# Weight sums in DRAM handed out from the end of the first products, not in attention alone

## The chip, the cores and the metric

The kernel runs on one core of one Trainium2 chip. The metric is the device time in microseconds (us) of one execution. TensorE (PE, with its weight loads PEld) multiplies, VectorE (DVE), ScalarE (ACT) and GpSimd (POOL) work on tiles, and SyncE (SP) issues most of the transfers. POOL issues the others, all those that add to what lies at their destination. PE and SP follow the order in which the program is written, in all of the kernel. In the stretch that this change touches, DVE, ACT and POOL do so too. An instruction that waits holds up everything that stands behind it on its engine.

## The reference, cut to what matters

One layer with sliding-window attention, an output projection, and a gated embedding, for 512 tokens of width 2048:

```python
hn = rmsnorm(x, norm_g)
q, k, v, gate = split(hn @ w_in)         # 32 heads of 64, 4 key/value heads
s = q @ k.T * 64 ** -0.5 + bias          # window of 128 keys; bias by distance, 32 buckets, from rel_bias
m = max(s.max(-1), sink)                 # one more score per head, the "sink"
p = exp(s - m) / (exp(s - m).sum(-1) + exp(sink - m))
x = x + ((p @ v) * silu(gate)) @ w_out
emb = p_in @ ple_proj
x = x + emb * sigmoid(rmsnorm(x, ple_norm) @ ple_gate)
out = rmsnorm(x, final_g)
```

## The kernel before, in words

**Products.** Every large product is done as three matmuls on a high and a low part (`mm3`, lines 126 to 128). A piece of weights, 128 x 1024 numbers or 512 KB, is loaded by SP into a `wraw` tile (line 102), cast by ACT to its high part `whi` (line 109), and subtracted by DVE to its low part `wlo` (line 110). There are three buffers of each. The load of piece i+1 is issued when the split of piece i is handed out, and the load of piece 3 needs the buffer of piece 0, which is free when DVE has made `wlo` of piece 0.

**Stages.** First come the first products: 16 steps that make queries of the first two heads, all keys and values. `W.load(3)` and `W.get(0)` then load pieces 0 to 3 and split 0 to 2. `W.get(0)` ends with the load of piece 3 on SP. Behind it the program prepares keys and values, and POOL builds the table of biases: it loads `rel_bias` into `misc` (line 381), clears the table (382), fills it with 17 small copies (385, 390) and writes it to DRAM as `tdram` (392). SP reads the biases of the first heads back from `tdram` into a `bias` tile (`load_bias(0)`, line 444, four transfers). Then the projections run as a generator, one step of three matmuls (one of 16 parts of a product) at a time: 16 steps alone, and after that 64 blocks of attention between which the remaining steps are dealt out. A block is, in this order on the engines: two matmuls of scores (PE, line 462); on POOL, the sink into a column of the tile `t` (line 474) and a fill of masked places (477); on DVE, bias and scores added into `t` (482, 484 for the first two blocks) and the maximum taken (491); two exponentials on ACT (495); a reciprocal on DVE (497); a scaling on ACT into `pr` (506); one block later a transpose of `pr` on PE (515). The tile of scores has one buffer, so PE's scores of a block wait until DVE has read the scores of the block before. After attention come the output projection and the gated embedding (`ple_gate`).

**The sums.** Both late products use seven products in place of eight (sums of blocks of weights and of activations). The sums of weights are made in DRAM: a copy on SP (`copies`, line 662, DRAM to DRAM, 512 KB) and then an addition of another block into it on POOL (`adds`, line 664, 512 KB). There are 56 of each. `sum_weights(i)` does step i of 118: copy i/2 where i is even, and addition (i-1)/2 - 3 where i is odd, so an addition is handed out behind three copies later than its own. An addition waits on POOL for its copy to land. The first ten copies belong to `w_out` 7 (`small` twice, then eight pieces); their first use is in the output projection. Before the change each block of attention hands out its share of the 118 steps at the end of the block:

```python
for n in range(i * SUM_STEPS // blocks, (i + 1) * SUM_STEPS // blocks):
    sum_weights(n)
```

Of the kernel before, what the change touches and what calls it, by code (L numbers as in the profile page):

```python
# [11 lines left out]
F32 = mybir.dt.float32  # L12
F32R = mybir.dt.float32r
AF = mybir.ActivationFunctionType
ALU = mybir.AluOpType
# [5 lines left out]
P = 128  # L21
# [34 lines left out]
def trunk_kernel(ctx: ExitStack, tc: tile.TileContext, a: dict):  # L56
    nc = tc.nc
# [28 lines left out]
    WE = 1024  # L86
# [71 lines left out]
    def run(gen):  # L158
        for _ in gen:
            pass  # L160
# [34 lines left out]
    pre = ExitStack()  # L195
    start_pool = pre.enter_context(tc.tile_pool(name="start", bufs=3))

    front = ExitStack()
    for k in range(KC):
        if k == 0:  # L200
# [35 lines left out]
        if k == 0:  # L236
            first, second = slice(0, 1), slice(1, 2)
# [19 lines left out]
        f, e = k == 0, k == KC - 1  # L257
# [13 lines left out]
        for t in range(2):  # L271
            c = slice(t * P, (t + 1) * P)
            mm3(kt_ps[t], wh[:, c], wl[:, c], h, l, f, e)

        for part in "hl" if f else "lh":
            for t in range(NB):
                c = slice(t * P, (t + 1) * P)
# [6 lines left out]
        if 3 <= k < 3 + NB:  # L284
            t = k - 3
# [12 lines left out]
            nc.sync.dma_start(pn, a["ple_norm"])  # L298
    W.load(3)
    W.get(0)  # L300

    Q = {}

# [82 lines left out]
    for b in range(exact, BUCKETS):  # L386
        d = np.nonzero(bk == b)[0]
        if len(d):
            lo, n = P - 1 + int(d.min()), len(d)
# [37 lines left out]
    def first_chores(i, step):  # L427

        if step == 0 and i < NB - 1:
            make_diff(i + 1)  # L430
        if step and 1 <= i < NB:
            diffs[i][step - 1]()
        if step == 2 and 1 <= i - 1 < NB:
            spread_diff(i - 1)
        if step and 1 <= i - 2 < NB:
            split(V[i - 2], values[i - 2])[step - 1]()
# [71 lines left out]
    def turn(i):  # L508


        d, g = divmod(i, UNITS)
        pr = T.pop(i)
        pt = bank(f"pt{i}", "t")[:, :256]
        for u in range(2):
            nc.tensor.transpose(pt[:, u * P : (u + 1) * P], pr[:, u, :], ident)  # L515

        r = apool.tile([P, 2, 256], F32R, tag="r", name=f"r{i}", bufs=2)
        rh, rl = (r[:, l].rearrange("p (h u q) -> p u h q", h=4, u=2) for l in range(2))
        src = pt.rearrange("p (u h q) -> p u h q", u=2, h=4)
        nc.scalar.copy(rh, src)  # L520
        nc.vector.tensor_sub(rl, src, rh.bitcast(F32))  # L521
        yield
        own = None
        if g >= 2:
            own = apool.tile([P, 2, 256], F32R, tag="own", name=f"own{i}", bufs=2)
            rows = slice(0, P) if g % 2 else slice(0, HB)
            flat = lambda v: v[rows].rearrange("p l (u q) -> p (l u) q", q=HB)


            sign = -1 if g % 2 else 1  # L530
            nc.gpsimd.affine_select(  # L531
                out=flat(own), in_=flat(r).bitcast(F32), pattern=[[0, 8], [sign, HB]], compare_op=ALU.is_ge, fill=0.0,
                base=-HB - 1 if g % 2 else 0, channel_multiplier=-sign,
            )
        PT[i] = (r, own)
        yield
        if own is not None:
            here, there = slice(HB, P), slice(0, HB)
            if g % 2 == 0:
                here, there = there, here  # L540
            nc.scalar.copy(own[there, 0], own[here, 1].bitcast(F32))
# [85 lines left out]
        (4, 0): {0: 5, 1: 5, 2: 4, 3: 4}, (4, 1): {0: 3, 1: 3},  # L627
    }

    summed, copies, adds = {}, [], []

    def block(nm, r, c, jj, m):
        return a[nm][2 * (c - 1) + jj, 4 * (r - 1) + m]

    SUMS = [("w_out", 7), ("w_out", 5), ("w_out", 6), ("w_out", 4), ("ple_gate", 7), ("ple_gate", 5)]

    def small_block(r, c, m):

        return block("w_out", 2, 1, c - 1, 2 * (r - 1) + m)

    for (nm, p), small in zip(SUMS, (7, 5, 6, 4, None, None)):
        for m in range(2 if small else 0):
            t = summed["small", small, m] = tc.dram_tile([P, WE], F32, name=f"small_{small}_{m}")
            copies.append((t, {
                7: small_block(1, 2, m), 5: small_block(1, 1, m), 6: summed.get(("small", 7, m)),
                4: summed.get(("small", 6, m)),
            }[small]))
            adds.append((t, small_block(*{7: (2, 2), 5: (1, 2), 6: (1, 1), 4: (2, 1)}[small], m)))  # L650
        for jj in range(2):
            for m in range(4):
                t = summed[nm, p, jj, m] = tc.dram_tile([P, WE], F32, name=f"{nm}_{p}_{jj}_{m}")
                first = {7: (1, 2), 5: (1, 1)}.get(p)
                copies.append((t, block(nm, *first, jj, m) if first else summed[nm, {6: 7, 4: 6}[p], jj, m]))
                adds.append((t, block(nm, *{7: (2, 2), 5: (1, 2), 6: (1, 1), 4: (2, 1)}[p], jj, m)))
    SUM_STEPS = 2 * len(copies) + 6

    def sum_weights(i):

        if i % 2 == 0 and i // 2 < len(copies):
            nc.sync.dma_start(*copies[i // 2])
        elif i % 2 == 1 and 0 <= i // 2 - 3 < len(adds):
            nc.gpsimd.dma_start(*adds[i // 2 - 3], accum_op=ALU.add, max_dma_last_dim=8192)

    class Pieces:


# [70 lines left out]
    def add_stage(nm, order):  # L739
# [7 lines left out]
        for p in order:  # L747
            for jj in range(2):
# [5 lines left out]
                for m in range(4):  # L754
                    at[p, jj].append(len(B.specs))
                    if (nm, p) in SUMS:
                        src = summed[nm, p, jj, m]
# [90 lines left out]
    W.apart = True  # L848
    for n in range(KC):
        next(proj)  # L850
        if n % 4 == 3 and W.todo:
            W.todo.pop(0)()
    blocks = TWOS * UNITS
    left = KC * (len(kinds) - 1)

    def some(of, n=1):
        for _ in range(min(n, len(of))):
            of.pop(0)()

    softmax = iter(())  # L860
    for i in range(blocks + 3):

        before, softmax = softmax, scores(i) if i < blocks else iter(())
        turned = turn(i - 2) if 2 <= i < blocks + 2 else iter(())
        value = weigh(i - 3) if 3 <= i else iter(())
        next(turned, None)
        next(value, None)
        next(softmax, None)
        next(turned, None)
        next(before, None)  # L870
        next(softmax, None)
        first_chores(i, 0)
        if i in (6, 20, 36):
            idle.extend(make_key(1 + i // 16))
        todo = left // (blocks + 2 - i) if i < blocks + 2 else 0
        left -= todo
        for n in range(max(todo, 6)):
            if n < todo:
                next(proj)
            if n == 0:  # L880
                first_chores(i, 1)
                some(W.todo)
                some(chores or idle)
            elif n == 2:
                next(value, None)
                if len(chores) > 1:
                    some(chores)
            elif n == 3:
                next(turned, None)
                next(softmax, None)  # L890
            elif n == 4:
                first_chores(i, 2)
                some(chores or idle)
            elif n == 5:
                next(softmax, None)
        if i < blocks:
            for n in range(i * SUM_STEPS // blocks, (i + 1) * SUM_STEPS // blocks):
                sum_weights(n)
    for _ in proj:
        pass  # L900
    while chores or idle:
# [171 lines left out]
    for n, p in enumerate(ORDER_OUT):  # L1073
        nxt = out_forms.steps(ORDER_OUT[n + 1]) if n < 5 else iter(())
        for jj in range(2):
            later.extend(held.pop(waiting.get((p, jj)), ()))
            calls = iter(range(4))

            def between(m):
                q = small_steps.get((p, jj, m))  # L1080
                if q is not None:
                    next(small_made.setdefault(q, small_form(q)))
                q = SMALL.get((p, jj), {}).get(m)
                if q is not None:
                    small(q)

            def todo():
                step = next(calls)
                part = x_at.get((p, jj, step))
                if part is not None:  # L1090
                    load_x(part)
                next(nxt, None)
                if p == 4:

                    for _ in range({0: 2, 1: 2, 2: 2, 3: 2, 6: 2, 7: 2}.get(4 * jj + step, 0)):
                        turn(*turns.pop(0), "o")
                    if jj:
                        next(ple_first, None)

            ps = unit(p, jj, at_out, out_forms, todo, between)  # L1100
            posts = [partial_of(add_y, p, jj, tb, ps[tb]) for tb in range(2)]
            if p == 1:
                held[p, jj] = posts
            else:
                later.extend(posts)
        run(nxt)
        if p == 3:
            nc.sync.dma_start(fg, a["final_g"].partition_broadcast(P))
        if p == 3:
            turns = [(kp, th) for kp0, th in ((4, 1), (4, 0), (0, 0)) for kp in range(kp0, kp0 + 4)]  # L1110
# [144 lines left out]
    f = ple_forms.made[4]  # L1255
# [74 lines left out]
    n = done[3]  # L1330
# [87 lines left out]
```

## Time and profile before

| | us |
|---|---|
| median of 3 runs | 796.1 (795.71 to 797.07) |
| the profiled execution, its time | 794.62 |
| its span, first to last instruction | 792.9 |
| PE busy | 782.9 (99%) |
| DVE busy | 600.3 (76%) |
| ACT busy | 507.1 (64%) |
| POOL busy | 122.2 (15%) |

The granted TensorE clock of the profiled execution is 0.997. In the profile, SPq rows are transfers that SP issues, and "us to landing" of a transfer counts from its issue to the last of its 16 engines. The first products end near 71 us, the first block of attention starts near 82 us, and the output projection's first product starts near 440 us.

### The profile page before, as it was taken

The page shows a single profiled execution, that of the slowest core. Times are in us where ns is not written, and L with a number is a line of the kernel's source. Part 1 is how long each engine was busy: PE and PEld are TensorE (multiplying, and loading weights), DVE is VectorE, ACT ScalarE, POOL GpSimd, SP SyncE. Part 2 cuts the span into 40 slices and gives each one's busy share as a digit, 9 for nine tenths or more (in the row PEclk, how much of TensorE's full clock was granted, in tenths as well). Part 3 has the DMA queues.
Part 4 walks back from the last instruction along what each step waited for, and adds up shares of the span by engine and source line. Part 5 has one row for each costly group of instructions (what it writes and reads, how often), then busy time and mean ns, then how long its engine had stood idle before and what let it go on. Part 6 is the DMA issues. An engine that isn't in the chain of part 4 may idle for free.

```text
span 792.9 us, 11070 instructions
## 1 busy us (share of the span) xinstructions
PE 782.9 (99%) x3746; PEld 655.1 (83%) x3746; DVE 600.3 (76%) x1043; ACT 507.1 (64%) x1066; POOL 122.2 (15%) x246
## 2 busy tenths in 40 slices
PE   9999999999999999999999999999999999999995
PEld 8888888888888888888888888888888888888885
DVE  4546697877878687877777899778867757988896
ACT  6742576666767586666666654466698656656765
POOL 0020223131323213132222100000000120200000
PEclk9999999999999999999999999999999999999998
DMA  9883499899999989998997369767764995787633
GB/s 352 281 212 132 116 271 316 243 277 235 278 257 267 250 254 272 228 280 238 260 259 187 107 236 393 300 210 235 275 236 140 347 206 195 160 226 216 182 107 106
DMA packets 45577, 185.22 MB, mean 234 GB/s; under 512 B 6656, under 2 KB 7680, under 8 KB 40400
## 3 DMA queue, kind: packets, MB, share of 16 engines
q1 hardware_dynamic: 37984, 145.40, 52.2%
q0 software_dynamic: 7536, 39.12, 26.1%
q8 instruction: 29, 0.48, 0.3%
q14 instruction: 28, 0.23, 0.1%
HBM read 177.63 MB, written 62.97 MB: 303 GB/s over the span
## 4 chain that ended last, share of the span: by engine, by line
PE 91%; DVE 4%; DMA 2%; ACT 1%; issue 1%; ACTq 0%; SPq 0%; DVEq 0%
PE qps L126 7%; PE qps L128 7%; PE qps L127 7%; PE gps L126 7%; PE gps L128 7%; PE gps L127 7%; PE g L126 5%; PE g L127 5%; PE g L128 5%; PE o L127 4%; PE o L126 4%; PE o L128 4%; PE s L462 2%; PE vps L279 2%; DVE blo L701 2%; PE o L557 2%
## 5 line engine op out<-in xcount | busy, mean ns | idle before, releaser
L701 DVE TENSOR_TENSOR blo<-braw,bhi 128x1024 fp32r<-128x1024 f32 x102 | 124.3, 1221 | 40.9 <-ACT bhi L700 40.6
L700 ACT CAST bhi<-braw 128x1024 fp32r<-128x1024 f32 x102 | 107.1, 1051 | 70.0 <-PE o L128 23.6
L126 PE MATMUL gps<-xh,whi 128*128 128x512 f32 x256 | 99.8, 390 | 0.1
L128 PE MATMUL gps<-xh,wlo 128*128 128x512 f32 x256 | 99.9, 390 | 0.0
L127 PE MATMUL gps<-xl,whi 128*128 128x512 f32 x256 | 99.8, 390 | 0.0
L126 PE MATMUL qps<-xh,whi 128*128 128x512 f32 x224 | 87.7, 391 | 0.0
L128 PE MATMUL qps<-xh,wlo 128*128 128x512 f32 x224 | 87.5, 390 | 0.0
L127 PE MATMUL qps<-xl,whi 128*128 128x512 f32 x224 | 87.3, 390 | 0.0
L110 DVE TENSOR_TENSOR wlo<-wraw,whi 128x1024 fp32r<-128x1024 f32 x60 | 73.8, 1232 | 2.9 <-ACT whi L109 2.5
L126 PE MATMUL g<-bhi,fhg 128*128 128x512 f32 x192 | 75.1, 391 | 0.0
L127 PE MATMUL o<-blo,fho 128*128 128x512 f32 x192 | 74.8, 390 | 0.2 <-DVE blo L701 0.2
L126 PE MATMUL o<-bhi,fho 128*128 128x512 f32 x192 | 74.8, 390 | 0.0
L128 PE MATMUL g<-bhi,flg 128*128 128x512 f32 x192 | 74.8, 389 | 0.0
L128 PE MATMUL o<-bhi,flo 128*128 128x512 f32 x192 | 74.7, 389 | 0.0
L127 PE MATMUL g<-blo,fhg 128*128 128x512 f32 x192 | 74.7, 389 | 0.0
L531 POOL TENSOR_SCALAR_AFFINE_SELECT own<-r 64x512 fp32r<-64x512 f32 (+1 forms) x48 | 32.5, 677 | 245.6 <-DVE r L521 245.6
L520 ACT CAST r<-pt 128x256 fp32r<-128x256 f32 x64 | 23.8, 371 | 71.7 <-PE pt L515 71.3
L521 DVE TENSOR_TENSOR r<-pt,r 128x256 fp32r<-128x256 f32 x64 | 27.1, 424 | 55.8 <-ACT r L520 54.9
L109 ACT CAST whi<-wraw 128x1024 fp32r<-128x1024 f32 x60 | 62.3, 1040 | 5.4 <-issue 3.9
L128 PEld LDWEIGHTS gps<-xh,wlo 128*128 128x128 f32 x256 | 48.0, 188 | 10.1
L126 PEld LDWEIGHTS gps<-xh,whi 128*128 128x128 f32 x256 | 48.1, 188 | 9.4 <-PE vps L279 0.5
L495 ACT ACTIVATE t<-t,sm 128x129 f32<-128x129 f32 x128 | 50.6, 397 | 8.0 <-DVE sm L491 6.4
(224 smaller groups left out, 1740.8 us busy)
## 6 DMA issues: line engine op xcount, KB each, us to landing
wraw<-in_w_gate_in SPq DMA_DIRECT2D x32, 512.0 KB, 6.9
w_out<-in_w_out POOLq DMA_DIRECT2D x32, 512.0 KB, 8.6
braw<-w_out SPq DMA_DIRECT2D x32, 512.0 KB, 4.6
wraw<-in_w_q SPq DMA_DIRECT2D x28, 512.0 KB, 6.3
braw<-in_ple_gate SPq DMA_DIRECT2D x24, 512.0 KB, 3.4
braw<-in_w_out SPq DMA_DIRECT2D x22, 512.0 KB, 4.3
xw<-in_first SPq DMA_DIRECT2D x14, 640.5 KB, 6.3
w_out<-in_w_out SPq DMA_DIRECT2D x16, 512.0 KB, 8.5
```

The lines of the kernel that those rows point to most:

```text
L109: nc.scalar.copy(hi, raw)
L110: nc.vector.tensor_sub(lo, raw, hi.bitcast(F32))
L126: nc.tensor.matmul(ps, sh, mh, start=first, stop=False, skip_group_check=more)
L127: nc.tensor.matmul(ps, sh, ml, start=False, stop=False, skip_group_check=more)
L128: nc.tensor.matmul(ps, sl, mh, start=False, stop=last, skip_group_check=more)
L279: nc.tensor.matmul(v_ps[t], h[:, c], both[:, :, 256:512], start=f, stop=e, skip_group_check=True)
L495: nc.scalar.activation(su, su, AF.Exp, bias=sm[:, u : u + 1], accum_out=sm[:, 2 + u : 3 + u])
L520: nc.scalar.copy(rh, src)
L521: nc.vector.tensor_sub(rl, src, rh.bitcast(F32))
L531: nc.gpsimd.affine_select(out=flat(own), in_=flat(r).bitcast(F32), pattern=[[0, 8], [sign, HB]], compare_op=ALU.is_ge, fill=0.0, base=-HB ...
L700: nc.scalar.copy(hi, raw)
L701: nc.vector.tensor_sub(lo, raw, hi.bitcast(F32))
```

## The change

The functions and the lists move ahead of the first products, unchanged. The steps are then taken in order by `sum_some(n)` from one iterator: 8 steps behind `W.get(0)`, 8 steps during the 16 projection steps ahead of attention, 96 steps in attention's 64 blocks, and the last 6 one at a time in the output projection's first product.

```diff
+    sum_steps = iter(range(SUM_STEPS))
+
+    def sum_some(n):
+        for _, i in zip(range(n), sum_steps):
+            sum_weights(i)
 ...
     W.load(3)
     W.get(0)
+    sum_some(8)
 ...
     load_bias(0)
     W.apart = True
     for n in range(KC):
         next(proj)
+        if n % 2:
+            sum_some(1)
         if n % 4 == 3 and W.todo:
             W.todo.pop(0)()
 ...
         if i < blocks:
-            for n in range(i * SUM_STEPS // blocks, (i + 1) * SUM_STEPS // blocks):
-                sum_weights(n)
+            sum_some((i + 1) * (SUM_STEPS - 22) // blocks - i * (SUM_STEPS - 22) // blocks)
 ...
                 if part is not None:
                     load_x(part)
                 next(nxt, None)
+                sum_some(1)
                 if p == 4:
```

On the engines of the built kernel this gives the following. PE, DVE and ACT carry the same instructions in the same order as before. On SP, copies 0 to 3 stand between the load of piece 3 and the biases' four transfers. Copies 4 to 6 stand between those and the load of piece 4, copy 7 between the loads of pieces 4 and 5, and copies 8 and 9 ahead of that of piece 6. On POOL, addition 0 stands ahead of the load into `misc`, with which the table of biases begins. Additions 1 to 4 stand between the writing of `tdram` and the sink of the first block (line 474). The last three additions, 53 to 55, stand behind attention.

More of the change, by code (lines that the diff above doesn't have):

```diff
@@ L196, in trunk_kernel, with block, small_block, sum_weights @@
     start_pool = pre.enter_context(tc.tile_pool(name="start", bufs=3))
+    summed, copies, adds = {}, [], []
+    def block(nm, r, c, jj, m):
+        return a[nm][2 * (c - 1) + jj, 4 * (r - 1) + m]
+    SUMS = [("w_out", 7), ("w_out", 5), ("w_out", 6), ("w_out", 4), ("ple_gate", 7), ("ple_gate", 5)]
+    def small_block(r, c, m):
+        return block("w_out", 2, 1, c - 1, 2 * (r - 1) + m)
+    for (nm, p), small in zip(SUMS, (7, 5, 6, 4, None, None)):
+        for m in range(2 if small else 0):
+            t = summed["small", small, m] = tc.dram_tile([P, WE], F32, name=f"small_{small}_{m}")
+            copies.append((t, {
+                7: small_block(1, 2, m), 5: small_block(1, 1, m), 6: summed.get(("small", 7, m)),
+                4: summed.get(("small", 6, m)),
+            }[small]))
+            adds.append((t, small_block(*{7: (2, 2), 5: (1, 2), 6: (1, 1), 4: (2, 1)}[small], m)))
+        for jj in range(2):
+            for m in range(4):
+                t = summed[nm, p, jj, m] = tc.dram_tile([P, WE], F32, name=f"{nm}_{p}_{jj}_{m}")
+                first = {7: (1, 2), 5: (1, 1)}.get(p)
+                copies.append((t, block(nm, *first, jj, m) if first else summed[nm, {6: 7, 4: 6}[p], jj, m]))
+                adds.append((t, block(nm, *{7: (2, 2), 5: (1, 2), 6: (1, 1), 4: (2, 1)}[p], jj, m)))
+    SUM_STEPS = 2 * len(copies) + 6
+    def sum_weights(i):
+        if i % 2 == 0 and i // 2 < len(copies):
+            nc.sync.dma_start(*copies[i // 2])
+        elif i % 2 == 1 and 0 <= i // 2 - 3 < len(adds):
+            nc.gpsimd.dma_start(*adds[i // 2 - 3], accum_op=ALU.add, max_dma_last_dim=8192)
+    sum_steps = iter(range(SUM_STEPS))
+    def sum_some(n):
+        for _, i in zip(range(n), sum_steps):
+            sum_weights(i)
     front = ExitStack()
@@ L628, in trunk_kernel @@
     }
[L632 to L664, printed above, removed]
     class Pieces:
```

## The prediction

> **What bounds the kernel now.** I read the windows first, to see in which stage PE has time to give or none. The columns are each engine's busy us (and instructions), then the granted clock, the DMA share and GB/s.
>
> ```profile
> core 0: us, PE busy (x) PEld busy (x) DVE busy (x) ACT busy (x) POOL busy (x), PEclk, DMA share, GB/s
> 70.00:95.00 25.00, 24.93 (x114) 20.40 (x113) 18.19 (x39) 11.09 (x25) 6.12 (x11) 1.00 0.28 90
> 95.00:440.00 345.00, 345.00 (x1709) 290.43 (x1708) 266.62 (x589) 232.31 (x643) 89.97 (x182) 1.00 0.93 255
> 440.00:700.00 260.00, 259.72 (x1181) 215.08 (x1180) 205.16 (x236) 166.70 (x249) 15.93 (x18) 1.00 0.73 234
> 700.00:793.00 93.00, 84.13 (x400) 70.71 (x398) 76.00 (x115) 58.33 (x86) 3.44 (x4) 0.98 0.53 166
> ```
>
> PE is busy in every us of attention (95 to 440), although the DMA engines are at 0.93 there. From 70 to 700 it is idle for 0.07 + 0.00 + 0.28 = 0.35 us. The waits of PE, asked for next, say the same: after the start there is one.
>
> ```profile
> PE warm_ps L141 <- PEq L1408: 0.8, 1, 0.8
> PE o L127 <- DVE blo L701: 0.2, 1, 0.2
> ```
>
> So PE sets the time, at full clock, and nothing that lightens the transfers in attention can give back more than 0.35 us, unless it reaches the last stage with its 8.87 us of idle time, in which no sum of weights is made. Whatever delays PE anywhere is lost for good. The quiet stretch is 70 to 95: DMA share 0.28. The change moves work there. The question is whether something on which PE soon depends stands behind that work. I then followed SP and POOL instruction by instruction from 40 to 95 us, and from their landings to PE.
>
> **The change part by part.** *The fewer steps in attention* (96, not 118) and *the last three additions*, in the output projection on a POOL that is nearly idle (15.93 us busy in 260), remove nothing that PE waits for. I cost them at nothing: cover is PE's unbroken 345.00, and the last pieces, of `ple_gate`, are wanted only in the stage after.
>
> *The four copies behind the load of piece 3.* That load starts when DVE has finished the low part of piece 0:
>
> ```profile
> 56.68 1.23 DVE L110 TENSOR_TENSOR wlo<-wraw,whi 128x1024 fp32r<-128x1024 f32 x1 [1.79 <-ACT whi L109]
> 57.93 0.33 SPq L102 DMA_DIRECT2D wraw<-in_w_q  x1
> 62.55 1.72 SPq L444 DMA_DIRECT2D bias<-tdram  x4
> 64.37 0.84 SPq L102 DMA_DIRECT2D wraw<-in_w_q  x2
> 65.27 1.27 SPq L662 DMA_DIRECT2D small<-in_w_out  x2
> ```
>
> 57.93 + 0.33 gives 58.3 for copy 0, and at 1.27 / 2 = 0.63 each the four are issued by 60.8, before SP could start on the biases (62.55). On SP this costs nothing. What matters is when copy 0 lands, since POOL waits for it. Landings, in the order in which I use them (the last number is us from issue):
>
> ```profile
> w_out<-in_w_out SPq DMA_DIRECT2D x1, 512.0 KB, 4.0
> small<-in_w_out SPq DMA_DIRECT2D x2, 512.0 KB, 7.4
> small<-in_w_out POOLq DMA_DIRECT2D x1, 512.0 KB, 6.7
> ple_gate<-in_ple_gate POOLq DMA_DIRECT2D x1, 512.0 KB, 5.1
> w_out<-in_w_out POOLq DMA_DIRECT2D x32, 512.0 KB, 8.6
> misc<-in_rel POOLq DMA_DIRECT2D x1, 4.0 KB, 5.0
> tdram<-misc POOLq DMA_DIRECT2D x1, 48.0 KB, 5.3
> bias<-tdram SPq DMA_DIRECT2D x4, 20.0 KB, 1.8
> ```
>
> A copy alone took 4.0 (issued at 91.47), the two behind two loads 7.4. Copy 0 goes behind one load: I take the middle, 5.7, so it lands at 64.0 (62.3 to 65.7).
>
> *Addition 0 ahead of the table of biases.* Before, POOL did this:
>
> ```profile
> 44.20 0.53 POOL L381 DMA_DIRECT2D misc<-in_rel  x1
> 44.72 0.44 POOL L382 MEMSET misc<- 32x384 f32 x1
> 49.33 0.65 POOL L385 COPY misc<-misc 32x16 f32<-32x16 f32 x1 [4.17 <-DMA misc<-in_rel]
> 52.30 0.51 POOL L392 DMA_DIRECT2D tdram<-misc  x1 [0.29 <-DMA xw<-in_first]
> 62.60 0.18 POOL L474 COPY t<-sinkb 128x2 f32<-128x2 f32 x1 [9.78 <-PE vps L279]
> ```
>
> `tdram` was issued at 52.30 and landed at 57.6, five us before SP could use it. Now POOL waits at addition 0 until 64.0, and line 381, the memset, the 17 copies and line 392 all wait behind it. The load into `misc` moreover follows a 512 KB addition in POOL's one queue. That addition lands after 6.7 us (as the first one of attention, beside other traffic), at 70.7; between a lone one's 5.1 and the 8.6 median of attention it is 68.2 (there the 5.0 of `misc` itself ends last) to 74.3. `misc` lands just behind, at 70.9. From the landing of `misc` (44.20 + 5.0 = 49.2) to the issue of `tdram` (52.30) it took 3.1: 74.0. With its own 5.3, `tdram` lands at **79.3**. The ends: with 1.8, what a small transfer took in quiet, 68.2 + 3.1 + 1.8 = 73.1, and 74.3 + 0.2 + 3.1 + 5.3 = 82.9.
>
> *The load of piece 4.* SP waits for `tdram` at the biases, and behind them stand copies 4 to 6 and this load: 79.3 + 1.72 + 3 x 0.63 = 82.9 (76.7 to 86.5), where it was 64.4 before. How long it takes to land depends on what is in flight: three copies just ahead of it, and additions 1 to 3, which POOL issues right behind `tdram` as their copies have long landed. Its price:
>
> ```profile
> wraw<-in_w_q SPq DMA_DIRECT2D x2, 512.0 KB, 4.5
> wraw<-in_w_q SPq DMA_DIRECT2D x1, 512.0 KB, 8.2
> wraw<-in_w_q SPq DMA_DIRECT2D x1, 512.0 KB, 11.8
> q1 hardware_dynamic: 37984, 145.40, 52.2%
> q0 software_dynamic: 7536, 39.12, 26.1%
> ```
>
> 4.5 with nothing ahead (64.37), 8.2 behind a copy and small transfers beside an addition (106.55), 11.8 when the queues were full (108.02). I take 8.2: landing at **91.1**. The queues' totals agree: 145.40 MB in 52.2% of 792.9 us is 1.49 us per 512 KB on all engines, and 39.12 MB in 26.1% is 2.77 per addition. Three additions and four SP transfers are 8.3 + 6.0 = 14.3 us of work; begun at about 76 they end at 90. The ends are 76.7 + 4.5 = 81.2 and 86.5 + 11.8 = 98.3.
>
> *Who waits for piece 4.* ACT's cast of it stands ahead of the first exponentials, so everything of blocks 0 and 1 follows it:
>
> ```profile
> 81.85 1.05 ACT L109 CAST whi<-wraw 128x1024 fp32r<-128x1024 f32 x1 [3.89 <-issue]
> 83.23 1.50 DVE L110 TENSOR_TENSOR wlo<-wraw,whi 128x1024 fp32r<-128x1024 f32 x1
> 87.00 0.70 ACT L506 ACTIVATE pr<-t,sm 128x128 f32<-128x128 f32 x2 [0.23 <-DVE sm L497]
> 87.26 0.46 DVE L482 TENSOR_TENSOR t<-s,bias 128x96 f32<-128x96 f32 x2 [0.29 <-PE s L462]
> 87.63 0.45 DVE L484 TENSOR_TENSOR t<-s,t 128x96 f32<-128x96 f32 x2
> 91.84 0.38 PE L515 MATMUL pt<-ident,pr 128*128 128x128 f32 x2
> 91.97 0.39 PE L462 MATMUL s<-k,q 128*128 128x320 f32 x1
> ```
>
> From the cast's start, `pr` of block 0 is there 87.70 - 81.85 = 5.85 later, and the scores of block 1 are read 88.08 - 0.29 - 81.85 = 5.94 later (without the 0.29 spent waiting for PE). PE wants them at 91.84 and 91.97. So piece 4 may land as late as **86.0** for nothing, and each us beyond it stops PE for one. Piece 4 itself is multiplied later still.
>
> Sum: 91.1 - 86.0 = **5.1 us** at the transposes and scores near 92 us, then nothing more: DVE, with 18.19 us busy of 25, needs only to follow, and the loads behind move with PE. On the profiled execution 794.62 + 5.1 = 799.7; on the median, which lies 1.5 above it, 796.1 + 5.1 = **801.2**. By the ends the stop is 0 to 12.3.
>
> **The rivals.**
>
> *The transfers in the quiet stretch are quick, and nothing stops.* It needs piece 4 by 86.0, so `tdram` by about 76, 3 us earlier than in my sum. For it: the DMA share of 0.28, and the low end of 81.2. Against: all the moved transfers are in that very stretch. Time 796.1; not slower. The decision lies at 86.0. [...]
>
> *POOL's sink is what comes last.* Addition 4 waits on POOL for copy 4, which SP issues behind the biases at 81.0, and the first sink (line 474) stands behind. With 7.4 for the copy it lands at 88.4, and 0.51 of issue (as line 392's) and 0.18 of line 474 later DVE may take the maximum, at 89.1 instead of 82.89:
>
> ```profile
> 82.89 0.42 DVE L491 TENSOR_REDUCE sm<-t 128x2 f32<-128x258 f32 x1
> ```
>
> 87.70 - 82.89 = 4.8 us after it, `pr` is there: 93.9 against 91.84 is a stop of 2.1, and 798.2. It decides if piece 4 lands before 88.1.
>
> *A second stop.* The load of piece 6 has copies 7 to 9 and the load of piece 5 ahead of it, and additions 4 to 7 beside it. With 1.49 and 2.77 us each, that is 5 x 1.49 + 4 x 2.77 = 18.5 us behind piece 4, at 109.6. Before, ACT cast it here:
>
> ```profile
> 99.17 1.05 ACT L109 CAST whi<-wraw 128x1024 fp32r<-128x1024 f32 x1
> ```
>
> With the 5.1 lost already, and room like that of piece 4 (86.0 - 81.85 = 4.15), it may land at 108.4. Another 1.2 would be lost: 802.4. It decides at 108.4. Against it: additions 5 to 7 wait for copies 5 to 7 and so come late themselves, and in attention loads took 11.8 us without a wait of PE.
>
> *Faster by relief.* Worth at most 0.35 us by the first table; only the last stage could give more, and no moved step is near it. That the change does not take place can be left out: the built order on SP and POOL shows it.
>
> **How the numbers follow.** Piece 4 late, with a stop of 1.6 to 10 us: 0.52. The sink, 1.6 to 4: 0.15. The second stop on top: 0.08. The far end, over 10: 0.07. Nothing stops, or under 1.6: 0.14. Faster: 0.04. A difference of 0.2%, 1.6 us, is about what a measurement of this kernel can tell from none. So faster 0.04, same 0.14, slower 0.82. The range goes from 796.0, which takes in the quick transfers, to 806.0, which leaves out the far end up to 12.3; with the faster cases about 1 in 10 lies outside, which I keep, since the landings of so many transfers at once are no row of this trace.
>
> **What would show it.** Right: POOL's wait for copy 0 until about 64 ahead of line 381's load; SP's wait for `tdram` until about 79; ACT waiting for piece 4 until about 91; PE idle some 5 us between 87 and 98, and none after it. Wrong: `tdram` landing before 76, or PE's idle time elsewhere, at the pieces of 100 to 125 us or in the output projection. A shorter time than before would refute the reading that PE had nothing to gain.

## The result, and the profile after

The changed kernel took 804.73 us (median of six runs, 803.68 to 806.95). The kernel before, run beside it, took 797.01 (six runs, 795.71 to 799.33). The ratio is 1.0101, with a 95% interval of 1.0080 to 1.0123: slower by 1%. The forecast was 801.2 with a range of 796.0 to 806.0. The profiled execution took 804.14 (span 802.4), where the forecast for it was 799.7. So it is 9.52 us longer than the profiled execution before (794.62), where 5.1 was forecast.

**Where PE stands still.** First the waits of PE in the changed kernel (total, times, longest), without the wait at the start, which is as before:

```profile
PE pt L558 <- ACT pr L549: 4.9, 1, 4.9
PE o L602 <- ACT own L584: 1.8, 2, 1.1
```

The transposes of block 0 (line 515 before, 558 now) wait 4.9 us for ACT's `pr`, as forecast. Two smaller waits at line 602 come on top. The windows say where, and show something that no wait shows. The columns are busy us (and instructions) of PE, PEld, DVE, ACT and POOL, then the granted clock, the DMA share and GB/s.

```profile
70.00:92.00 22.00, 21.93 (x101) 17.96 (x100) 11.32 (x23) 3.60 (x6) 9.75 (x32) 1.00 0.74 199
92.00:97.40 5.40, 0.53 (x3) 0.11 (x2) 3.23 (x8) 4.25 (x9) 3.80 (x5) 0.76 1.07 288
97.40:102.00 4.60, 4.57 (x14) 3.79 (x15) 3.54 (x10) 3.96 (x14) 1.15 (x3) 0.54 0.96 296
102.00:140.00 38.00, 36.20 (x176) 30.00 (x175) 29.99 (x65) 26.21 (x72) 6.59 (x16) 1.00 0.99 294
140.00:440.00 300.00, 300.00 (x1488) 252.64 (x1487) 229.21 (x510) 199.46 (x553) 68.86 (x154) 1.00 0.84 226
440.00:700.00 260.00, 259.88 (x1188) 215.57 (x1187) 203.57 (x242) 167.52 (x259) 16.85 (x20) 1.00 0.74 238
```

The stretch that was quiet, with a DMA share of 0.28, now has 0.74. After the stop PE counts as fully busy from 97.4 to 102, but with 14 matmuls at a granted clock of 0.54: work at about half speed (matmuls start 0.43 us apart up to 101.4, and 0.23 in the trace before), hidden in the column of busy time. Two gaps, 38.00 - 36.20 = 1.80 us in all, lie between 102 and 140. From 140 to 700 there are 0.12 us of idle time, so the fewer steps in attention and the late additions cost nothing.

**The way to the stop.** The timeline of POOL and SP in the changed kernel (start, length, in brackets the idle time before it and what ended that):

```profile
58.07 1.24 SPq L229 DMA_DIRECT2D small<-in_w_out  x2
65.17 0.86 POOL L231 DMA_DIRECT2D small<-in_w_out  x1 [21.42 <-DMA small<-in_w_out]
74.26 0.51 POOL L435 DMA_DIRECT2D tdram<-misc  x1 [0.29 <-POOL misc L433]
76.12 1.78 SPq L487 DMA_DIRECT2D bias<-tdram  x4
77.95 1.76 SPq L229 DMA_DIRECT2D w_out<-in_w_out  x3
79.81 0.53 SPq L102 DMA_DIRECT2D wraw<-in_w_q  x1
84.69 1.46 SPq L229 DMA_DIRECT2D w_out<-in_w_out  x2
87.06 0.33 SPq L102 DMA_DIRECT2D wraw<-in_w_gate_in  x1
87.28 0.77 POOL L231 DMA_DIRECT2D w_out<-in_w_out  x1 [10.00 <-DMA w_out<-in_w_out]
```

Line 231 is now the addition, 229 the copy, 435 the writing of `tdram`, 487 the biases. POOL waits 21.42 us at addition 0, and the table is written at 74.26, where it was 52.30. The landings of these transfers, from the view of transfers (the last number is us from issue):

```profile
small<-in_w_out SPq DMA_DIRECT2D x1, 512.0 KB, 6.8
small<-in_w_out POOLq DMA_DIRECT2D x1, 512.0 KB, 6.2
tdram<-misc POOLq DMA_DIRECT2D x1, 48.0 KB, 1.8
bias<-tdram SPq DMA_DIRECT2D x4, 20.0 KB, 7.0
wraw<-in_w_q SPq DMA_DIRECT2D x1, 512.0 KB, 12.4
wraw<-in_w_gate_in SPq DMA_DIRECT2D x1, 512.0 KB, 22.4
```

Piece 4, issued at 79.81, lands 12.4 later, at 92.2; piece 6, issued at 87.06 behind copies 8 and 9 (the row at 84.69), 22.4 later, at 109.5. ACT and PE in the timeline:

```profile
92.31 1.04 ACT L109 CAST whi<-wraw 128x1024 fp32r<-128x1024 f32 x1 [13.83 <-DMA wraw<-in_w_q]
96.88 0.69 ACT L549 ACTIVATE pr<-t,sm 128x128 f32<-128x128 f32 x2 [0.23 <-DVE sm L540]
97.43 0.67 PE L558 MATMUL pt<-ident,pr 128*128 128x128 f32 x2 [4.90 <-ACT pr L549]
104.73 0.38 PE L558 MATMUL pt<-ident,pr 128*128 128x128 f32 x2
109.50 1.05 ACT L109 CAST whi<-wraw 128x1024 fp32r<-128x1024 f32 x1 [2.79 <-DMA wraw<-in_w_gate_in]
117.19 0.39 PE L602 MATMUL o<-own,DV 128*128 128x256 f32 x1 [0.75 <-ACT own L584]
135.63 0.39 PE L602 MATMUL o<-own,DV 128*128 128x256 f32 x1 [1.05 <-ACT own L584]
```

From one block's transposes to the next PE took 104.73 - 97.43 = 7.30 us. In the trace before the same step is 97.15 - 91.84 = 5.31 (that block's transposes start at 97.15). PE had no idle time in this step, and the granted clock was 0.5 (half clock) until 101.6, so half clock lost 1.99.

**The sum of the difference.** I took the start of the same matmuls in both traces. The first matmul behind the first products is 0.53 later (71.38 against 70.85). The transposes of block 0 are 5.05 later beyond that. Half clock makes it 7.05, the wait at 117.19 makes it 8.12, the one at 135.63 makes it 9.42. Over the rest 0.4 comes back, near 493 us of the trace before, where PE had waited for `blo`, and 9.0 + 0.53 is the whole 9.52. About 54% of what was lost behind the start is thus the stop that was forecast.

### The profile page after: what moved, and what is told of

The parts are those of the page before. It is cut to its first block, busy times and chain, and to the rows that moved or that the text cites. A ratio compares the mean times of both kernels' runs of the same rounds, so it can differ in the third digit from the quotient of the medians.

```text
span 802.4 us, 11066 instructions
## 1 busy us (share of the span) xinstructions
PE 785.9 (98%) x3746; PEld 657.3 (82%) x3746; DVE 599.6 (75%) x1043; ACT 507.1 (63%) x1066; POOL 117.0 (15%) x246
## 4 chain that ended last, share of the span: by engine, by line
PE 85%; DMA 8%; DVE 3%; ACT 2%; issue 1%; POOL 0%; SPq 0%; ACTq 0%; DVEq 0%; POOLq 0%
PE gps L128 6%; PE gps L127 6%; PE gps L126 6%; PE qps L126 6%; PE qps L128 6%; PE qps L127 6%; PE g L128 5%; PE g L127 5%; PE g L126 5%; PE o L126 5%; PE o L127 5%; PE o L128 5%; DMA wraw<-in_w_gate_in 4%; PE s L505 2%; PE o L600 2%; PE pt L558 2%
## 5 line engine op out<-in xcount | busy, mean ns | idle before, releaser
L109 ACT CAST whi<-wraw 128x1024 fp32r<-128x1024 f32 x60 | 62.3, 1040 | 17.9 <-DMA wraw<-in_w_q 13.8
L127 PEld LDWEIGHTS gps<-xl,whi 128*128 128x128 f32 x256 | 48.1, 188 | 8.9
```

The source lines that it names most:

```text
L109: nc.scalar.copy(hi, raw)
L127: nc.tensor.matmul(ps, sh, ml, start=False, stop=False, skip_group_check=more)
```

## The experiments

The theory at the outset was the prediction's, mended by the first trace: `tdram` is late because it stands behind addition 0, everything on SP stands behind the biases, piece 4 lands too late, and PE's stop brings half clock on top. The rivals: the transfers that are handed out early are too many for this stretch, whatever their order; or POOL's sink, not piece 4, is what binds. Edits are against the changed kernel. Ratios are against the kernel before on the same chip.

| | kernel | us | ratio (95%) |
|---|---|---|---|
| 1 | addition 0 behind the table | 799.84 | 1.0041 (1.0020 to 1.0062) |
| 2 | piece 4's load ahead of the biases | 808.36 | 1.0128 (1.0104 to 1.0151) |
| 3 | stop filled with matmuls | 811.00 | 1.0160 (1.0135 to 1.0185) |
| 4 | late parts alone | 797.15 | 1.0000 (0.9983 to 1.0018) |
| 5 | the changed kernel again | 807.61 | 1.0141 (1.0122 to 1.0159) |
| 6 | first eight steps alone | 796.87 | 1.0006 (0.9992 to 1.0021) |
| 7 | no sums in blocks 0 to 5 | 806.44 | 1.0115 (1.0094 to 1.0137) |
| 8 | the same, stop filled | 803.23 | 1.0086 (1.0067 to 1.0104) |
| 9 | copies without additions | 799.84 | 1.0032 (1.0008 to 1.0055) |
| 10 | second eight steps alone | 798.55 | 1.0004 (0.9982 to 1.0027) |
| 11 | 1 and 7 together | 795.45 | 0.9992 (0.9975 to 1.0009) |
| 12 | piece 4's load behind the biases | 807.71 | 1.0135 (1.0108 to 1.0161) |

Kernels 1 to 4 ran on one chip, 5 to 8 on a second, and 9 to 12 on that second one at another time.

### 1. Addition 0 behind the table

Seven steps go out behind piece 0 instead of eight, so that addition 0 is the first step of the projections; attention has one more.

```diff
-    sum_some(8)
+    sum_some(7)
 ...
-            sum_some((i + 1) * (SUM_STEPS - 22) // blocks - i * (SUM_STEPS - 22) // blocks)
+            sum_some((i + 1) * (SUM_STEPS - 21) // blocks - i * (SUM_STEPS - 21) // blocks)
```

> Steps 0 to 6 (copies 0 to 3) stay behind the split of the first pieces; step 7, addition 0, is handed out with the next eight in the projection steps, so the table of biases stands ahead of every addition on POOL. My theory (addition 0 ahead of the table holds back the biases, and with them everything behind them on SP): tdram lands near 58 as before, piece 4 is issued near 67 and lands before 77, PE has no stop, 796 to 797.5. Rival (early copies and additions cost by their traffic alone, wherever they stand): most of the 7.7 us stays, 802 to 805.

Measured: 799.84, ratio 1.0041 (1.0020 to 1.0062). From its timeline, the issue of `tdram` and that of piece 4, and three casts on ACT; and from its waits of PE:

```profile
57.72 0.51 POOL L435 DMA_DIRECT2D tdram<-misc  x1 [0.29 <-POOL misc L433]
71.61 0.35 SPq L102 DMA_DIRECT2D wraw<-in_w_q  x1
85.86 1.05 ACT L109 CAST whi<-wraw 128x1024 fp32r<-128x1024 f32 x1 [7.07 <-DMA wraw<-in_w_q]
121.67 1.04 ACT L109 CAST whi<-wraw 128x1024 fp32r<-128x1024 f32 x1 [3.36 <-DMA wraw<-in_w_q]
PE o L602 <- ACT own L584: 4.0, 2, 3.4
```

The table is early again, and the stop at block 0 is gone. Piece 4, issued 8 us earlier than in the changed kernel, still took 14.2 us and came 0.2 ahead of its latest time of 86.0. The stop has moved: piece 9 is cast at 121.67 after a wait, and PE waits 3.4 us at line 602. So the late table is needed for the stop at 92 us, but it is not the whole cost: the queue of transfers remains, and bites later. The time lies between the two numbers expected, so neither theory is the whole.

### 2. Piece 4's load ahead of the biases

```diff
+    W.load(5)
     load_bias(0)
```

> As the changed kernel, but the load of piece 4 is issued on SP ahead of the biases. If piece 4's landing makes the first stop: no wait of ACT for it; PE stops only for POOL's sink, which stays behind addition 4, by 0.5 to 2 us near 92. What then becomes of the total tells two theories apart. Losses add (5.1 at piece 4, 2.0 by the half clock after it, 2.3 at piece 6): about 800. One debt (DVE, late by piece 6 at 109.5, sets the total whatever PE lost before): piece 6 has one load of 1.5 us less ahead of it, so about 803.

Measured: 808.36, ratio 1.0128 (1.0104 to 1.0151). Neither number was met. Piece 4 was there in time (cast at 81.86 without a wait for it). But the biases, four transfers of 20 KB, now came last, as DVE's row shows, and PE waited for DVE's reading of the scores and, later, three times more (twice at line 602, and 1.3 us at line 126):

```profile
89.62 0.32 DVE L525 TENSOR_TENSOR t<-s,bias 128x32 f32<-128x32 f32 x2 [8.86 <-DMA bias<-tdram]
PE s L505 <- DVE t L527: 3.4, 1, 3.4
PE o L602 <- ACT own L584: 4.0, 2, 3.2
```

The first of them was issued at 79.93, and the last had landed 9.6 us later, at 89.5. With piece 4 out of the way the next in line took its place. That speaks for the rival of too many transfers, and against piece 4 as the only cause.

### 3. The stop filled with matmuls

Twenty-two matmuls that nothing reads stand ahead of block 0's transposes, 22 x 0.228 = 5.0 us of work, in the stop (in the trace they take 5.15 us, from 95.30).

```diff
-        pt = bank(f"pt{i}", "t")[:, :256]
+        pt = bank(f"pt{i}", "t")
+        for _ in range(22 if i == 0 else 0):
+            nc.tensor.matmul(pt, xh[0][:, :P], xh[1], start=True, stop=True)
+        pt = pt[:, :256]
```

> As the changed kernel, with 22 more matmuls of 128x512 (results unused) on PE ahead of the first block's transposes, 5.0 us of work in the place where PE stands still. The granted clock should not fall to half behind it. Losses add: 2.0 us less than the changed kernel, about 802.7. One debt (piece 6 lands at 109.5 whatever PE does): the time stays 804.7 within 0.6, and PE's wait for the mask near 116 grows from 0.8 to about 3 us. If the half clock has another cause, it stays and nothing else changes.

Measured: 811.00, ratio 1.0160 (1.0135 to 1.0185); neither number was met. The granted clock is 1.00 in the windows from 85 to 140 us, with stops of at most 2.4 us. But piece 4 landed at 96.5 in this run, 4 us later than in the changed kernel's first trace, and the changed kernel did not run beside it. So it says nothing on the price. Experiment 8 repeats it with a partner.

### 4. The late parts alone

No steps ahead of attention; 112 in it, 6 in the output projection.

```diff
-    sum_some(8)
 ...
-        if n % 2:
-            sum_some(1)
 ...
-            sum_some((i + 1) * (SUM_STEPS - 22) // blocks - i * (SUM_STEPS - 22) // blocks)
+            sum_some((i + 1) * (SUM_STEPS - 6) // blocks - i * (SUM_STEPS - 6) // blocks)
```

> No step ahead of attention; 112 steps in the 64 blocks, the last 6 in the output projection's first product, as in the change. My theory: these parts cost and bring nothing, 796 to 797, all PE-busy in attention. Rival: the additions in the output projection, where DVE is busy 28.4 of 30 us, cost up to 1 us there.

Measured: 797.15, ratio 1.0000 (0.9983 to 1.0018). The late additions cost and bring nothing that the medians show. There is no cost without the 16 early steps. The profiled execution (799.54) has one wait of PE that was not expected, 3.3 us at line 601 near 438 us; experiment 10 comes back to it.

### 5. The changed kernel again

It ran beside experiments 6 to 8, unchanged.

> The changed kernel once more, on the chip of the next three, as their mark: 1.008 to 1.014 of the kernel before. The first four runs showed that tdram lands between 76 and 80 from run to run, and piece 4 between 92 and 96.5 where its copies stand ahead of it; the stop near 92 should be that landing less 86.4, 5 to 10 us.

Measured: 807.61, ratio 1.0141 (1.0122 to 1.0159). On this chip the cost comes out larger than in the first comparison (1.0101, interval to 1.0123); the intervals meet at their ends. Its profiled execution has the same stops: 5.8 us at block 0, and 1.9 in two waits at line 602.

### 6. The first eight steps alone

```diff
-        if n % 2:
-            sum_some(1)
 ...
-            sum_some((i + 1) * (SUM_STEPS - 22) // blocks - i * (SUM_STEPS - 22) // blocks)
+            sum_some((i + 1) * (SUM_STEPS - 14) // blocks - i * (SUM_STEPS - 14) // blocks)
```

> Steps 0 to 7 as in the change (copies 0 to 3 and addition 0 ahead of the table of biases), none in the projection steps, 104 in attention. So the table is as late as in the change (tdram at 76 to 80), but neither copies 4 to 6 nor additions 1 to 4 stand ahead of piece 4 and the sink. If the table alone makes the stop, it stays at 5 us or more, 803 to 806. My theory (the table is only the delay; what costs is the queue of copies and additions that is handed out behind it and ahead of pieces 4 to 6): piece 4 lands 4 to 5 us behind tdram, at 81 to 85, PE stops for 0 to 2 us, 796 to 799.

Measured: 796.87, ratio 1.0006 (0.9992 to 1.0021). From its timeline and its windows:

```profile
77.49 0.51 POOL L435 DMA_DIRECT2D tdram<-misc  x1 [0.29 <-POOL misc L433]
85.66 1.05 ACT L109 CAST whi<-wraw 128x1024 fp32r<-128x1024 f32 x1 [7.25 <-DMA wraw<-in_w_q]
85.00:95.00 10.00, 10.00 (x48) 8.34 (x47) 6.11 (x16) 7.82 (x19) 2.09 (x5) 1.00 1.04 288
```

The table is even later here than in the changed kernel (77.49 against 74.26), and it costs nothing: the biases come 1.8 us after their issue and piece 4 in 4.4, since neither copies nor additions are in flight ahead of them. ACT casts piece 4 at 85.66, against the 86.0 that the prediction gave as its latest time, and PE is busy for 10.00 of 10 us. The deadline holds from this side. A late table alone is free here, by 0.4 us. The profiled execution, 798.48, has two waits at line 602 later on, 2.0 in all. The medians show no difference to the kernel before.

### 7. No sums in blocks 0 to 5

Attention's 96 steps are handed out in blocks 6 to 63.

```diff
-            sum_some((i + 1) * (SUM_STEPS - 22) // blocks - i * (SUM_STEPS - 22) // blocks)
+            if i >= 6:
+                sum_some((i - 5) * (SUM_STEPS - 22) // (blocks - 6) - (i - 6) * (SUM_STEPS - 22) // (blocks - 6))
```

> As the changed kernel, but blocks 0 to 5 of attention hand out no step (the 96 go to blocks 6 to 63), so copies 8 and 9 and additions 5 to 8 no longer stand ahead of or beside pieces 5 to 7. Piece 4 and the first stop stay as in the changed kernel, with the half clock behind it. If piece 6 sets the total (one debt): its landing moves from about 110 to about 100, the stops near 116 and 134 go, 2 to 3 us less than the changed kernel. If the first stop alone sets it: no difference over 1 us.

Measured: 806.44, ratio 1.0115 (1.0094 to 1.0137), beside 1.0141 (1.0122 to 1.0159) for the changed kernel: the intervals overlap, and the difference of the medians, 1.2 us, lies between the two numbers expected. The traces are clearer. Piece 6 landed at 98.6 instead of 110.1, and the two waits at line 602 are gone. The stop at block 0 stays, as does half clock. The waits and one window of experiment 7 first, then those of experiment 8:

```profile
PE pt L558 <- ACT pr L549: 5.6, 1, 5.6
95.00:105.00 10.00, 7.37 (x23) 6.06 (x24) 7.01 (x19) 7.52 (x23) 0.37 (x2) 0.66 0.63 185
```

```profile
PE pt L561 <- ACT pr L549: 1.0, 1, 1.0
95.00:105.00 10.00, 8.99 (x43) 7.15 (x42) 7.97 (x19) 7.81 (x23) 0.47 (x3) 1.00 0.71 202
```

At the eighth block's transposes the offset to the kernel before, counted as above, is 8.4 us here and 10.0 in experiment 5. So the second place, around piece 6, is made by copies and additions of attention's first blocks, and is worth 1.6 us in these two traces.

### 8. The same with the stop filled

The edit is that of experiment 3 and that of experiment 7 together.

> As the kernel without sums in blocks 0 to 5, with 22 more matmuls of 128x512 (results unused) on PE ahead of the first block's transposes, 5.0 us of work in the place of the stop. With no debt left at piece 6, the half clock is a loss of its own: 2.0 us less than the kernel without sums in blocks 0 to 5, and no half clock near 97. If a later landing still sets the total: no difference. If the stop is shorter than 5 us on this chip: up to as much slower as it is shorter.

Measured: 803.23, ratio 1.0086 (1.0067 to 1.0104), and 1.0115 (1.0094 to 1.0137) for its partner, with the upper end here above the lower end there by 0.0010. The medians say 3.2 us less, although PE has 5.0 us more to do, and piece 4 was cast 1.6 us later in the profiled execution (94.11 against 92.51). The mechanism shows in the trace. In the window above the granted clock is 1.00 with 43 matmuls begun, some of them the added ones, where experiment 7 has 0.66 with 23. From block 0's transposes to the next takes 104.70 - 99.23 = 5.47 us, in experiment 7 105.55 - 97.63 = 7.92, in the kernel before 5.31. So the step behind the stop is 2.6 us longer than before with half clock, and 0.2 without. That half clock follows this stop, and that filling the stop avoids it, is shown; the whole gain in the medians is only likely.

### 9. Copies without additions

During the projections only copies 4 to 7 are handed out. Additions 1 to 4 follow in blocks 6 to 9.

```diff
+    held = []
 ...
-        if n % 2:
+        if n % 4 == 1:
             sum_some(1)
+            held.append(next(sum_steps))
 ...
+            if i >= 6 and held:
+                sum_weights(held.pop(0))
```

> As the changed kernel, but the projection steps hand out copies 4 to 7 alone; their four additions (1 to 4) come in blocks 6 to 9. So the table is as late and the same three copies stand ahead of piece 4, but no addition runs beside them and none stands ahead of the sink. If the additions are what stretches piece 4 (12.4 to 13 us in the changed kernel): it lands 8 to 10 us behind tdram, at 85 to 88, the stop is 0 to 2 us with no half clock, 797 to 800. If the copies on its own queue do it: piece 4 stays at 91 or later and the time at 804 or more.

Measured: 799.84, ratio 1.0032 (1.0008 to 1.0055), in runs of 796.51 to 802.65. The profiled execution was the slowest of them, 802.65. In it:

```profile
77.16 0.51 POOL L435 DMA_DIRECT2D tdram<-misc  x1 [0.29 <-POOL misc L433]
bias<-tdram SPq DMA_DIRECT2D x4, 20.0 KB, 1.8
82.67 0.53 SPq L102 DMA_DIRECT2D wraw<-in_w_q  x1
91.39 1.05 ACT L109 CAST whi<-wraw 128x1024 fp32r<-128x1024 f32 x1 [13.44 <-DMA wraw<-in_w_q]
PE pt L558 <- ACT pr L549: 4.5, 1, 4.5
```

Behind the same late table the biases, now with nothing in flight ahead of them, take 1.8 us instead of 7.0, and piece 4, behind the same three copies, 8.6 instead of 12.4. With neither ahead of it it took 4.4 (experiment 6). So both kinds stretch it, by about 4 us each, and neither of the two expectations is the whole. This execution misses what was expected of the additions: piece 4 lands at 91.3, not by 88, PE stands still for 4.5 us, and half clock follows (a granted clock of 0.66 over 95 to 105 us). (One addition that attention's first blocks hand out was issued at 87.15, beside the end of this load.) By the medians, two thirds of the cost or more go with the additions (0.32% is left, of 1.0 to 1.4%). What is left fits the late table with three copies ahead of piece 4; a faster execution was not traced.

### 10. The second eight steps alone

```diff
-    sum_some(8)
 ...
-            sum_some((i + 1) * (SUM_STEPS - 22) // blocks - i * (SUM_STEPS - 22) // blocks)
+            sum_some((i + 1) * (SUM_STEPS - 14) // blocks - i * (SUM_STEPS - 14) // blocks)
```

> No step behind the split of the first pieces, so the table stands ahead of all; steps 0 to 7 (copies 0 to 3, addition 0) in the projection steps, 104 in attention. If both halves are needed for the cost: 796 to 798, no stop at the first block. If eight steps in the projection steps cost by themselves, in whatever place the table stands: 800 or more.

Measured: 798.55, ratio 1.0004 (0.9982 to 1.0027). Its table is written at 57.31, and ACT casts piece 4 without waiting for it, so block 0 has no stop:

```profile
82.47 1.05 ACT L109 CAST whi<-wraw 128x1024 fp32r<-128x1024 f32 x1 [3.88 <-issue]
438.62 0.38 PE L601 MATMUL o<-own,DV 128*128 128x256 f32 x1 [2.05 <-ACT own L583]
```

The second row is the longest of three late waits at line 601 in the profiled execution, 3.4 us in all. That execution took 800.52, in runs of 795.02 to 801.04. Experiment 4 has such a wait at the same place, the trace of the kernel before has none; what makes it is not shown, and no difference of the medians clear of noise goes with it. Experiments 6 and 10 together: either half of the early steps costs nothing that the medians show, both do. The cost is their meeting.

### 11. Addition 0 behind the table, and no sums in blocks 0 to 5

The edits of experiments 1 and 7, with 97 steps in blocks 6 to 63.

> As the kernel with addition 0 handed out later (1.0041), and blocks 0 to 5 hand out no step. That kernel still stood for 3.4 us near 121, behind piece 9. If its rest is a queue of sums ahead of pieces 6 to 9: this goes, 796 to 797.5. If it comes from the steps ahead of attention: 799 to 801 as it was.

Measured: 795.45, ratio 0.9992 (0.9975 to 1.0009). The one wait of PE behind the start, and piece 4; then the first addition on POOL, and the biases:

```profile
PE o L602 <- ACT own L584: 0.4, 1, 0.4
84.69 1.05 ACT L109 CAST whi<-wraw 128x1024 fp32r<-128x1024 f32 x1 [6.52 <-DMA wraw<-in_w_q]
64.53 0.86 POOL L231 DMA_DIRECT2D small<-in_w_out  x1 [6.96 <-DMA small<-in_w_out]
bias<-tdram SPq DMA_DIRECT2D x4, 20.0 KB, 6.1
```

Fifteen early steps are free if the table goes first and the first blocks are left quiet. This takes back the 0.4% of experiment 1, and gains nothing over the kernel before: there was nothing to gain. No version ran that beats the kernel before. The biases are worth a look: issued from 62.77 to 64.11, before any addition, they took 6.1 us behind copies 0 to 3, where they took 1.8 in experiments 6 and 9. Additions 0 and 1, issued at 64.53 and 66.23, ran beside the rest, so how much of the 6.1 the copies make alone is not shown.

### 12. Piece 4's load right behind the biases

```diff
     load_bias(0)
+    W.load(5)
```

> As the changed kernel, but the load of piece 4 stands on SP right behind the biases, ahead of copies 4 to 6; the additions stay. The reverse of the kernel with copies and without additions. If the copies stretch piece 4: it lands 5 to 7 us behind tdram, at 82 to 86, and what is left is the sink behind addition 4 and copy 4, 1 to 4 us of stop, 799 to 803. If the additions do: it lands at 88 or later, with 3 us or more of stop, 802 to 806.

Measured: 807.71, ratio 1.0135 (1.0108 to 1.0161). Piece 4 now has no copy between the biases and itself, and still took 9.8 us behind three additions. It lands at 90.7, as expected for the additions, but the time is above both ranges. PE waits at four lines instead of two. Besides the rows shown, it waits 2.4 us at line 126 and 1.8 at the transposes:

```profile
PE o L602 <- ACT own L584: 2.6, 2, 2.1
PE s L505 <- DVE t L527: 2.6, 1, 2.6
```

With experiment 2 it shows that moving one load ahead only changes which transfer comes last. What helped was to take transfers out of the stretch (6, 9, 10), or to let them begin earlier and stop earlier (11).

## Why the prediction was right, and where it was off

**Copy 0, addition 0, the table: right.** Copy 0 landed at 64.9 (forecast 64.0, 62.3 to 65.7), addition 0 started at 65.17 and took 6.2, `misc` landed at 71.6, 0.2 behind it, and `tdram` was issued at 74.26 (forecast 74.0). POOL's one wait in front of the building of the table was the cause forecast for it, and experiment 1 shows it by undoing it.

**`tdram` and piece 4: two sizes off that cancel.** `tdram` landed in 1.8, not in the 5.3 of its row before: the low end. So it landed at 76.05, and piece 4 went out at 79.81 instead of 82.9. But its price was 12.4, not 8.2: above even the upper end of 11.8. 91.1 was forecast and 92.2 came, by 3.1 too early and 4.2 too long: that it came so close is luck. What counted was the sum of everything in flight, which the prediction had only as its second way, the queues' totals (14.3 us of work from about 76, so 90). Experiments 6, 9 and 12 show the parts: 4.4 us with neither copies nor additions ahead, 8.6 behind the copies, 9.8 behind the additions, 12.4 with both.

**The deadline of 86.0 and the stop of 5.1: right.** 4.9 us of waiting (5.05 by the starts) came at the transposes named. The chain from the cast to `pr` took 97.57 - 92.31 = 5.26, where 5.85 was taken, and PE itself came 0.53 later, so a landing 1.1 later than forecast gave the same stop. That these cancel is luck too. Experiment 6, which lands at 85.6 and loses nothing, holds the deadline from the other side.

**"Then nothing more": the step that failed.** After the stop 1.99 us went in half clock, for which the prediction had no term; the windows of the kernel before, in which PE never stops up to the last stage, have 1.00 there. Then 1.07 and 1.17 followed at 117.19 and 135.63. This is the rival of a second stop: piece 6 landed at 109.5, where its sum said 109.6 and its limit 108.4. Its price of 1.2 was too small: PE met the delay twice, for 2.2 to 2.4 in all. Experiment 7, where piece 6 lands at 98.6, removes both waits by leaving the first blocks quiet. That ACT and DVE ran behind in between is likely, but no run separates it. The sign of the text's own test, PE's idle time at pieces of 100 to 125 us, was thus partly there, beside the main stop and not in its place.

**The other rivals.** The quick transfers did not come: the 512 KB of the rows above took 6.2 to 22.4, with others in flight, and piece 4 landed at 92.2, not by 86.0. POOL's sink was late as that rival had it (DVE's maximum at 88.5, forecast 89.1), and did not decide, since piece 4 came after 88.1. Relief was 0.4, against at most 0.35 forecast: PE's wait on `blo` is gone.

**The sum.** 5.05 + 1.99 + 1.07 + 1.17 makes 9.3; with 0.1 in small differences, 0.4 of relief and the 0.53 by which the first products ended later it is 9.5 on the profiled execution. On the medians the difference is 804.73 - 797.01 = 7.7, of which 5.1 was forecast.

## What to carry to other kernels

When work is moved into a quiet stretch, follow each queue that it is put on to the first small transfer behind it that somebody needs: here one waiting instruction on GpSimd held up a table of 48 KB, and the table SyncE's loads. Price a landing by all that is in flight at that time, not by the row of one transfer (piece 4 took 4.4 us with neither copies nor additions ahead, 12.4 with both), and ask whether two delays that are each free meet. A forecast stop of TensorE needs further terms: for the half clock that may follow it (1.99 us lost here behind 4.9, and it was also seen behind a stop of 2.05), and for a second late landing behind it (2.2 to 2.4 us here).

## What the runs showed of the hardware

**Half clock after a stop.** In the changed kernel the trace's record of the granted clock stands at 0.5 from 94.78 to 101.6, that is 6.83 us, and matmuls start 0.43 us apart instead of 0.23. The stop of 4.9 began at 92.53. Five other runs with long stops have a low clock behind them too: 0.66 over 95 to 105 us with the stops of 5.8 in experiment 5, 5.6 in experiment 7 and 4.5 in experiment 9, 0.72 over 85 to 95 with the 3.4 of experiment 2, and, in experiment 1, matmuls 0.43 us apart from 126.09 to 129.07 behind the stop of 3.4.

Shorter stops went both ways. In experiment 10 the matmuls from 439.90 to 442.89 start 0.43 us apart, behind the 2.05 of the row that ends at 438.62; in experiment 12 they do so from 90.31 to 93.30 behind a stop of 2.60, and from 121.09 to 124.08 behind one of 2.13. Between these two, behind a stop of 2.37 that ends at 115.30, they start 0.23 us apart, and so they do in experiment 3 behind one of 2.38 that ends at 90.20. The windows of experiments 10 and 3:

```profile
440.00:444.00 4.00, 4.00 (x13) 3.14 (x12) 3.53 (x8) 2.62 (x8) 1.38 (x2) 0.61 0.99 202
```

```profile
85.00:95.00 10.00, 7.62 (x35) 6.05 (x34) 1.00 (x5) 0.00 (x0) 3.76 (x10) 1.00 1.08 313
```

So in these runs the length of a stop alone does not tell whether half clock follows; what does is not shown.

**Small transfers behind others.** The four transfers of 20 KB for the biases took 1.8 us with nothing in flight ahead of them (experiments 6 and 9, where the copies follow them), 7.0 behind three additions (the changed kernel), and 6.1 behind copies 0 to 3, with additions 0 and 1 issued while they were under way (experiment 11). So in these runs the same small transfers took three to four times as long with large ones ahead of them.
